# One of sixteen weight-sum units moves from the mixer's last block to its second; the last stores go to two queues by turns

## The chip, the cores and the metric

The kernel runs on one core of one Trainium2 chip. The metric is the device time of one execution in microseconds (us), and for this kernel it is given as the median of three runs. The engines that matter are TensorE (PE in the profile, with its weight loads as PEld), VectorE (DVE), ScalarE (ACT), GpSimd (POOL) and SyncE (SP), which issues nearly all of the kernel's DMA transfers.

## The reference

One layer (DEPTH is 1) of a hybrid encoder runs on 2048 new tokens and 64 tokens of a running stream, in float32, with a model width of 1024:

```python
def hybrid_layer(x, ...):
    h = rmsnorm(x, norm1_w)
    proj = h @ w_in                       # q, k, v, z, a, b and pooling input
    ...                                   # short convolution, SiLU
    o, s_new = gated_delta_chunked(q, k, v, g, beta, s_prev, chunk)
    ...                                   # gated norm of o, multi-scale pooling
    x = x + jnp.concatenate([o_delta, o_pool], axis=-1) @ w_out
    h = rmsnorm(x, norm2_w)
    x = x + (jax.nn.silu(h @ w_gate) * (h @ w_up)) @ w_down
    return x, conv_new, s_new.astype(x.dtype), pool_new
# then y = rmsnorm(x, normf_w)
```

The first half (projection, delta rule, pooling, output projection) is called the mixer here, the second half (gate, up, down) the FFN.

## The kernel before, in words

**Layout.** Everything is held transposed: channels on the 128 partitions, tokens along the free dimension. A dense product is made of three passes: a number is split into a high part (a cast to fp32r on ACT) and a low part (a subtraction on DVE), and high x high, high x low and low x high are summed in PSUM. Each weight tile therefore needs one ACT cast and one DVE subtraction before TensorE can use it. Where a split weight is used again, it is stored in DRAM and loaded back already split.

**The mixer** runs over four blocks of 512 tokens; block 0 also takes the 64 running tokens. In each block the projections of 21 column tiles (`win`) alternate with the delta rule's chains of small products in float16 and float32, one chain per head; the output projection (`wout`) of one block runs inside the next. The output projections of the last two blocks end the mixer.

**The FFN** runs over three blocks of 704 tokens, each as two halves of 352. Gate, up and down use a seven-product scheme of Strassen's kind (buffers `px`, `py`, `pz` for gate and up, `dx`, `dy`, `dz` for down), which needs four sums of quarters of each weight tile: S1, S2, S3 and S4. The 22 hidden tiles are taken in groups of `FGROUPS = (4, 4, 4, 4, 2, 4)`.

**Weight-sum units.** For the down weights `wd` of the four groups named in `PRE[0]` = (1, 2, 3, 5) these sums are made during the mixer by `pre_sums("dn", f, i)`, four units to a group, 16 in all. A unit loads two pieces of `wd` of 128 x 512 (one into the constant tile `poolw`, which the profile calls `consts`, one into a buffer of the `pw` ring, `prdn` in the profile), makes four sums of 128 x 256 on POOL, splits each on ACT and DVE into a spare corner of the block's activation tiles (`h` or `op` in the profile), and stores the four results to `dsd`. The FFN loads them again in `load_down`. The landing place `poolw` exists once, so the next unit's load into it waits for the unit before. All these transfers are issued by SP.

**Where a unit stands.** `plan` is the list of weight tiles in the order in which TensorE uses them, and `with_pres` inserts a unit behind the keys whose places in the block's list are given by `PRE_AT`. `prep()` walks this list a few keys ahead of use (`AHEAD = 3`); a unit is noted at that point but hands no weight over. Blocks 1, 2 and 3 get five, six and five units.

**The order of instructions.** `Machine` records every operation and then issues them by a list schedule with costs of its own: per engine it takes the ready operation with the lowest rank. For TensorE it also holds on to fp32r work before it turns to float16 or float32 products. The order on each engine, and on SP's queue, is fixed in this way before the kernel runs, so that any change to the list of operations can change the order of others.

**The end.** The last FFN block's last down product is done in two halves (`halves`, `ENDS`). `last_norm` follows each: squares on ACT, sums on POOL, a column sum on TensorE, then eight scaled outputs of 128 x 352. In the second half (`i` = 1) six of them are made on DVE and the first two (`SHARE`) on POOL, and each is stored by `nc.sync.dma_start` as soon as it is there.

Of the kernel before, what the change touches and what calls it, by code (L numbers as in the profile page):

```python
# [18 lines left out]
P = 128  # L19
D = 1024  # L20
KT = D // P
# [19 lines left out]
TB2 = NTOK // NB2  # L41
# [10 lines left out]
PRE = (1,2,3,5),(1,2,3,5),(1,2,3)  # L52
# [317 lines left out]
def hybrid_kernel(ctx, tc, a, o):  # L370
    nc = machine = Machine(tc.nc)
# [10 lines left out]
    def mm(out, lhsT, rhs, start, stop, **kw):  # L382
        nc.tensor.matmul(out, lhsT, rhs, start=start, stop=stop, **kw)
        n = 1
        for d in out.shape[1:]:
            n *= d
        cost(n, rhs.dtype)
# [89 lines left out]
    for lo, n in S0:  # L477
        for i in range(2):
            nc.sync.dma_start(out=x0[i][:, :, lo : lo + n],
                              in_=a["xT"][4 * i : 4 * i + 4, :, lo : lo + n].rearrange("k p t -> p k t"))  # L480
# [17 lines left out]
    groups, f0 = [], 0  # L498
# [3 lines left out]
    plan, pres = [], []  # L502
    for gi, (f0, G) in enumerate(groups):
        pres += [("pre", "gu", f, i) for f in range(f0, f0 + G) if f in PRE_GU for i in range(2)]
        pres += [("pre", "dn", f0, m) for m in range(KT // 2) if gi in PRE[0]]

    def with_pres(j, keys):

        out = []
        for i, key in enumerate(keys):  # L510
            out.append(key)
            if i in PRE_AT.get(j, ()) and pres:
                out.append(pres.pop(0))
        return out

    for j in range(NBLK):
        win = [("win", m) for m in range(21)]
        base = len(plan)
        at = 5 + 4 * OUT_AFTER
# [40 lines left out]
    def wtiles(nm, second=False):  # L560

        pool, x = (wq["pool"], "2") if second else (wpool, "")
        at = state["at"]
        return (lambda: pool.tile([P, 512], F32, tag="wraw" + x, name=f"wr{nm}_{at}", bufs=3 if second else 4),
                lambda: pool.tile([P, 2, 512], F32R, tag="wsp" + x, name=f"ws{nm}_{at}", bufs=4))

    def wsplit(t, raw, n=512, eng=None):
        nc.scalar.copy(t[:, 0, :n], raw[:, :n])
        (eng or nc.vector).tensor_tensor(out=t[:, 1, :n], in0=raw[:, :n], in1=t[:, 0, :n].bitcast(F32), op=ALU.subtract)

    def prep():
        key = plan[state["at"]]
        state["at"] += 1
        if key[0] == "pre":
            return pre_sums(*key[1:])
# [83 lines left out]
    def pre_sums(what, f, i):  # L659

        n = 256
        (tl, tr), (ll, lr) = ([t[:, i * n : i * n + n] for i in range(2)] for t in (
            names["poolw"], gp.tile([P, PX], F32, tag="pw", name=f"pr{what}{f}_{i}", bufs=2)[:, :512]))
        if what == "dn":
            for t, m0 in ((tl, i), (ll, i + KT // 2)):
                both = bass.AP(t.tensor, t.offset, [list(t.ap[0]), [1, 2 * n]])
                nc.sync.dma_start(out=both, in_=a["wd"][m0][:, f * P : f * P + 2 * n])
            dst = dsd[f, i]
        else:
            for t, nm, at in ((tl, "wg", 0), (tr, "wg", 512), (ll, "wu", 0), (lr, "wu", 512)):  # L670
                nc.sync.dma_start(out=t, in_=a[nm][f][:, at + i * n : at + i * n + n])
            dst = gpd[f, i]
        gt = nc.gpsimd.tensor_tensor
        spare = B.spare + B.o_spare + (prev.o_spare if prev else [])
        gt(out=lr, in0=lr, in1=ll, op=ALU.add)
        gt(out=ll, in0=tl, in1=ll, op=ALU.subtract)
        gt(out=tl, in0=lr, in1=tl, op=ALU.subtract)
        gt(out=tr, in0=tr, in1=tl, op=ALU.subtract)
        for j, x in enumerate((ll, lr, tl, tr)):
            parts = spare[j % len(spare)]  # L680
            split_w(parts.rearrange("p (q n) -> p q n", q=2), x)
            nc.sync.dma_start(out=dst[j], in_=parts.bitcast(F32))

    def split_w(t, x):

        nc.scalar.copy(t[:, 0], x)
        tt(t[:, 1], x, t[:, 0].bitcast(F32), ALU.subtract)

    def load_down(m, f0, G):

        n, t = G // 2 * P, {}
        for i, nms in enumerate((("11", "12"), ("S3", "S1"), ("S2", "S4"), ("22",))):
            raw, part = wtiles(f"d{nms[0]}", i % 2 == 1)
            part = part()
            if nms[0][0] == "S":
                both = part.rearrange("p q n -> p (q n)").rearrange("p (j q n) -> p j q n", j=2, q=2)
                nc.sync.dma_start(out=both.rearrange("p j q n -> p j (q n)").bitcast(F32),
                                  in_=dsd[f0, m][2 * i - 2 : 2 * i].rearrange("j p n -> p j n"))
                t |= {nm: [both[:, j]] for j, nm in enumerate(nms)}
            else:  # L700
                raw, k = raw(), n * len(nms)
                src = a["wd"][m + (KT // 2 if i else 0)]
                nc.sync.dma_start(out=raw[:, :k], in_=src[:, (f0 + G) * P - k : (f0 + G) * P])
                wsplit(part, raw, k)
                t |= {nm: [part[:, :, j * n : j * n + n]] for j, nm in enumerate(nms)}
        return t

    def prep_down(m, f0, G):
# [214 lines left out]
    at = 0  # L923
# [614 lines left out]
    for k in (4, 5, 6, 7, 0, 1, 2, 3):  # L1538
        t = wpool.tile([P, 512], F32, tag="xc", name=f"od{k}", bufs=XBUFS["xc"])
# [23 lines left out]
    for nm in FH[3:]:  # L1563
        t = f2.tile([P, 4, 2, N2], F32R, tag=f"h{nm}", name=f"hB{nm}")
# [25 lines left out]
    def last_norm(b, ys, i, done):  # L1590

        lo, n = ENDS[i]

        def new(nm):
            return f2.tile([P, 2, N2], F32, tag="hr", name=nm, bufs=3).rearrange("p s n -> p (s n)")[:, :n] if n > N2 else tmp(nm)[:, :n]

        rf = new(f"rf{b}_{i}")
        if i:
            scaled, scales = [], f2.tile([P, 2, N2], F32, tag="hr", name="scales", bufs=3).rearrange("p s n -> p (s n)")
        for k in range(KT):  # L1600
            yield lambda: len(done) > k
            yield 0.8
            sq = rf if k == 0 else new(f"sq{k}nf{b}_{i}")
            act(sq, columns(ys[k], lo, n), AF.Square)
            if i and k < SHARE:
                scaled.append(scales[:, k * n : k * n + n])
                act(scaled[k], columns(ys[k], lo, n), AF.Copy, scale=nfw[:, k : k + 1])
            if 0 < k < KT - 1:
                nc.gpsimd.tensor_tensor(out=rf, in0=rf, in1=sq, op=ALU.add)
        if i == 0:  # L1610
            yield 1.5
        ps = psg(f"rpnf{b}_{i}")[:, :n]
        mm(ps, ones, rf, start=True, stop=False)
        mm(ps, ones, sq, start=False, stop=True)
        act(rf, ps, AF.Ln, bias=epsc, scale=1.0 / D)
        if i:
            act(ps, rf, AF.Exp, scale=-0.5)
        act(rf, rf, AF.Exp, scale=-0.5)
        for k in (*range(SHARE, KT), *range(SHARE)) if i else range(KT):
            y = columns(ys[k], lo, n)  # L1620
            if i and k < SHARE:
                nc.gpsimd.tensor_tensor(out=y, in0=scaled[k], in1=rf, op=ALU.mult)
            else:
                stt(y, y, nfw[:, k : k + 1], ps if i else rf, ALU.mult, ALU.mult)
            nc.sync.dma_start(out=o["yT"][k, :, b * TB2 + lo : b * TB2 + lo + n], in_=y)
            if i == 0:
                yield LAT_STAT

    def columns(y, lo, n):

        return y.rearrange("p s n -> p (s n)")[:, lo : lo + n]

    def tmp(nm):
        return f2.tile([P, N2], F32, tag="t", name=nm, bufs=TB)
# [125 lines left out]
    for op in order:  # L1760
        b = op[1]
        if op[0] == "gu":
            f = op[2]
# [5 lines left out]
            gi = max(g for g, (f0, G) in enumerate(groups) if f0 <= f)  # L1769
# [14 lines left out]
        else:  # L1784
            f0, G = groups[op[2]]
# [5 lines left out]
            for which in halves(b, op[2]) if plain(b, op[2]) else ():  # L1791
                done = []
                if which != (0, 1):
                    Chain(last_norm(b, ys[b], *which, done))
                down(b, op[2], hs, ys[b], which, done)
# [14 lines left out]

MARGIN = {"tensor": 0.25, "vector": 0.1, "scalar": 0.1, "gpsimd": 0.1, "sync": 3.0}
NY, NLEV, NOUT, NX = 3, 3, 5, 3
PRE_AT = {1:(4,8,12,16,20),2:(4,7,10,13,16,19),3:(3,6,9,12,15)}
PRE_GU = ()

XBUFS = {"xs": 4, "xc": 3}
# [138 lines left out]
```

## Time and profile before

| what | value |
|---|---|
| time, median of 3 runs | 2297.03 us (2296.47 to 2297.72) |
| the profiled execution's own time | 2296.7 us |
| its span, first to last instruction | 2294.9 us |
| mean granted TensorE clock | 0.999 |
| PE busy | 2272.2 us (99%), 14518 instructions |
| DVE busy | 1710.1 us (75%) |
| ACT busy | 1342.4 us (58%) |
| POOL busy | 829.9 us (36%) |
| HBM read, written | 403.62 MB, 130.58 MB |
| chain that ended last, share by engine | PE 91%, DVE 4%, DMA 2% |

The span is what the trace covers; the time is 1.8 us longer. In a row of instructions the first figure behind the count is the busy time in us and the second the mean of one in ns; what stands behind the next bar is the idle time of the engine just before these instructions, with what ended it. Almost every instruction is recorded by one helper and so has the line number L285; rows are told apart by their tiles. A row "A <- B" in a view of waits says that A waited for B, with the total in us, the number of times and the longest. Matmuls overlap, so the pitch from one to the next is shorter than the mean duration of one.

Stages on the trace's clock, read from the tiles: block 0 of the mixer 9 to 198 us, block 1 198 to 430, block 2 430 to 650, block 3 650 to about 860, the last output projection to 935, the FFN to 2284, and the last norm and stores to the end.

### The profile page before, as it was taken

How to read it: one execution, taken by the hardware profiler on the slowest of the kernel's cores; microseconds unless marked ns; L12 is line 12 of the kernel's file. 1: busy time of each engine (PE TensorE's matmuls, PEld its weight loads, DVE VectorE, ACT ScalarE, POOL GpSimd, SP SyncE). 2: the span in 40 equal slices, each digit the busy share in tenths (PEclk: the TensorE clock that was granted, in tenths of full speed). 3: DMA queues.
4: the chain of work that ended last, by engine and by line, in shares of the span. 5: the costliest groups of instructions: out<-in, count | busy, mean ns of one | idle time of the engine just before them, and what ended most of it. 6: DMA issues, size and time to landing. Idle time of an engine off the chain costs nothing.

```text
span 2294.9 us, 41549 instructions
## 1 busy us (share of the span) xinstructions
PE 2272.2 (99%) x14518; PEld 2132.5 (93%) x14518; DVE 1710.1 (75%) x3129; ACT 1342.4 (58%) x3039; POOL 829.9 (36%) x893
## 2 busy tenths in 40 slices
PE   8999999999999999999999999999999999999998
PEld 8998898888787888999999999999999999999998
DVE  7989866685678886788888787866667768666576
ACT  6987866684769874565446366554334574353344
POOL 3425342453247450565443245622111453010112
PEclk9999999999999999999999999999999999999999
DMA  8765687578477777877776578789766786667663
GB/s 291 263 185 190 202 293 234 189 236 273 160 243 241 201 213 256 301 257 245 260 265 240 189 253 302 247 261 318 230 199 198 262 272 230 209 216 224 210 194 105
DMA packets 256515, 536.96 MB, mean 234 GB/s; under 512 B 30001, under 2 KB 94001, under 8 KB 256305
## 3 DMA queue, kind: packets, MB, share of 16 engines
q1 hardware_dynamic: 256304, 534.30, 71.0%
q8 instruction: 114, 1.87, 0.3%
q14 instruction: 97, 0.79, 0.1%
HBM read 403.62 MB, written 130.58 MB: 233 GB/s over the span
## 4 chain that ended last, share of the span: by engine, by line
PE 91%; DVE 4%; DMA 2%; issue 1%; ACT 1%; POOL 0%; SPq 0%; DVEq 0%; ACTq 0%; POOLq 0%
PE px L285 22%; PE pp L285 18%; PE pz L285 13%; PE py L285 11%; PE dx L285 9%; PE dy L285 4%; PE d L285 3%; PE dz L285 2%; PE pk_p L285 2%; PE pt_p L285 2%; PE gr_p L285 1%; DVE y L285 1%; PE py_p L285 1%; DMA wnd<-wsp 1%; PE px_p L285 0%
## 5 line engine op out<-in xcount | busy, mean ns | idle before, releaser
L285 PE MATMUL pp<-h,wsp 128*128 128x512 f32 (+1 forms) x2480 | 548.5, 364 | 9.4 <-DVE wsp L285 9.4
L285 PEld LDWEIGHTS pp<-h,wsp 128*128 128x128 f32 x2480 | 401.8, 190 | 58.0 <-ACT wsp L285 9.1
L285 ACT CAST ws<-wr 128x512 fp32r<-128x512 f32 x198 | 122.2, 618 | 168.0 <-PE dx L285 55.4
L285 DVE TENSOR_TENSOR ws<-wr,ws 128x512 fp32r<-128x512 f32 x198 | 172.5, 875 | 31.1 <-ACT ws L285 27.4
L285 POOL TENSOR_TENSOR q<-hr,hr 128x352 f32<-128x352 f32 x52 | 57.9, 1114 | 372.7 <-DVE hr L285 369.9
L285 ACT CAST wsd<-wrd 128x512 fp32r<-128x512 f32 (+1 forms) x120 | 62.7, 526 | 176.7 <-PE dx L285 67.6
L285 DVE TENSOR_TENSOR y<-y,dx 128x352 f32<-128x352 f32 x240 | 121.6, 516 | 58.4 <-PE dx L285 57.6
L285 PE MATMUL pz<-op,wsp 128*128 128x288 f32 (+1 forms) x768 | 163.3, 353 | 0.1
L285 PE MATMUL px<-hA,ws 128*128 128x352 f32 x792 | 145.2, 322 | 0.0
L285 ACT ACTIVATE hr<-g 128x352 f32<-128x352 f32 x132 | 65.6, 497 | 131.2 <-DVE g L285 131.1
L285 PE MATMUL py<-hB,wsS 128*128 128x352 f32 x792 | 141.7, 322 | 0.0
L285 PE MATMUL py<-hA,wsS 128*128 128x352 f32 x792 | 141.3, 322 | 0.0
L285 PE MATMUL pz<-hB,ws 128*128 128x352 f32 x792 | 141.0, 322 | 0.0
L285 ACT CAST TV_p<-pt_p 128x512 f16<-128x512 f32 x192 | 110.2, 588 | 49.0 <-PE pt_p L285 48.6
L285 PE MATMUL px<-hA,wsS 128*128 128x352 f32 x792 | 138.2, 322 | 0.0
L285 PE MATMUL px<-hBT,wsS 128*128 128x352 f32 x792 | 138.0, 322 | 0.2 <-ACT g L285 0.2
L285 PE MATMUL px<-hBT,ws 128*128 128x352 f32 x792 | 137.8, 322 | 0.0
L285 PEld LDWEIGHTS pz<-op,wsp 128*128 128x128 f32 x768 | 120.9, 188 | 12.6 <-DMA wsp<-wod 0.6
L285 PEld LDWEIGHTS px<-hA,ws 128*128 128x128 f32 x792 | 130.0, 188 | 0.1
L285 PE MATMUL dy<-hq,wsdS 128*128 128x352 f32 x672 | 129.7, 322 | 0.3 <-DMA wsdS<-dsd 0.3
L285 PEld LDWEIGHTS py<-hA,wsS 128*128 128x128 f32 x792 | 129.4, 188 | 0.1
L285 PEld LDWEIGHTS px<-hBT,wsS 128*128 128x128 f32 x792 | 128.7, 188 | 0.9 <-ACT g L285 0.9
(697 smaller groups left out, 5771.7 us busy)
## 6 DMA issues: line engine op xcount, KB each, us to landing
wsS<-gS SPq DMA_DIRECT2D x176, 512.0 KB, 4.5
wsp<-wnd SPq DMA_DIRECT2D x126, 512.0 KB, 3.8
gS<-wsS SPq DMA_DIRECT2D x88, 512.0 KB, 5.1
wsdS<-dsd SPq DMA_DIRECT2D x88, 512.0 KB, 4.4
wr<-in_wg_dram SPq DMA_DIRECT2D x132, 256.0 KB, 3.8
wnd<-wsp SPq DMA_DIRECT2D x42, 512.0 KB, 5.5
wrd<-in_wd_dram SPq DMA_DIRECT2D x68, 256.0 KB, 2.8
xd<-x2d SPq DMA_DIRECT2D x96, 176.0 KB, 4.1
```

The lines of the kernel that those rows point to most:

```text
L285: getattr(getattr(self.nc, op.eng), name)(*args, **kw)
```

## The change

Three things change in the code.

1. `PRE_AT`: block 1 gets a sixth unit behind key 22 of its list, and block 3 has four units behind keys 2, 5, 8 and 11 in place of five behind 3, 6, 9, 12 and 15. Block 2 keeps its six places. The units keep their order, so that the first place of block 2 now holds the seventh unit where it held the sixth, and so on. Places count from 0.
2. `pre_sums` and `load_down` are written for groups of two tiles as well as four (`M = 4 // G`). `PRE` is unchanged and names groups of four only, so M is 1 and there are 16 units as before; but a unit now loads its four quarters by four transfers of 128 x 256 instead of two of 128 x 512.
3. In `last_norm`, the second half's stores of odd `k` are issued by ScalarE instead of SyncE.

```diff
-        pres += [("pre", "dn", f0, m) for m in range(KT // 2) if gi in PRE[0]]
+        pres += [("pre", "dn", f0, m) for m in range(KT // 2 * G // 4) if gi in PRE[0]]
...
         if what == "dn":
-            for t, m0 in ((tl, i), (ll, i + KT // 2)):
-                both = bass.AP(t.tensor, t.offset, [list(t.ap[0]), [1, 2 * n]])
-                nc.sync.dma_start(out=both, in_=a["wd"][m0][:, f * P : f * P + 2 * n])
+            G = dict(groups)[f]
+            M, c = 4 // G, G // 2 * P
+            for t, m0, at in ((tl, 0, 0), (tr, 0, c), (ll, KT // 2, 0), (lr, KT // 2, c)):
+                m0, at = m0 + i * M, at + f * P
+                nc.sync.dma_start(out=t.rearrange("p (m c) -> p m c", m=M),
+                                  in_=a["wd"][m0 : m0 + M, :, at : at + c].rearrange("m p c -> p m c"))
             dst = dsd[f, i]
...
     def load_down(m, f0, G):
 
-        n, t = G // 2 * P, {}
+        n, M, t = G // 2 * P, 4 // G, {}
...
-                t |= {nm: [both[:, j]] for j, nm in enumerate(nms)}
+                t |= {nm: [both[:, j, :, e * n : e * n + n] for e in range(M)] for j, nm in enumerate(nms)}
             else:
-                raw, k = raw(), n * len(nms)
-                src = a["wd"][m + (KT // 2 if i else 0)]
-                nc.sync.dma_start(out=raw[:, :k], in_=src[:, (f0 + G) * P - k : (f0 + G) * P])
-                wsplit(part, raw, k)
-                t |= {nm: [part[:, :, j * n : j * n + n]] for j, nm in enumerate(nms)}
+                raw, k, m0 = raw(), n * len(nms), m * M + (KT // 2 if i else 0)
+                src = a["wd"][m0 : m0 + M, :, (f0 + G) * P - k : (f0 + G) * P]
+                nc.sync.dma_start(out=raw[:, : k * M].rearrange("p (m c) -> p m c", m=M), in_=src.rearrange("m p c -> p m c"))
+                wsplit(part, raw, k * M)
+                t |= {nm: [part[:, :, e * k + j * n : e * k + j * n + n] for e in range(M)] for j, nm in enumerate(nms)}
...
-            nc.sync.dma_start(out=o["yT"][k, :, b * TB2 + lo : b * TB2 + lo + n], in_=y)
+            queue = nc.scalar if i and k % 2 else nc.sync
+            queue.dma_start(out=o["yT"][k, :, b * TB2 + lo : b * TB2 + lo + n], in_=y)
...
-PRE_AT = {1:(4,8,12,16,20),2:(4,7,10,13,16,19),3:(3,6,9,12,15)}
+PRE_AT = {1:(4,8,12,16,20,22),2:(4,7,10,13,16,19),3:(2,5,8,11)}
```

## The prediction

> **What bounds the kernel now.** I read the page's totals first, then the table by stage, then what TensorE waits for in the mixer. The totals:
>
> ```profile
> span 2294.9 us, 41549 instructions
> PE 2272.2 (99%) x14518; PEld 2132.5 (93%) x14518; DVE 1710.1 (75%) x3129; ACT 1342.4 (58%) x3039; POOL 829.9 (36%) x893
> ```
>
> TensorE is busy for 2272.2 of 2294.9 us, so all idle time on it comes to 22.7 us. No re-ordering of other engines can win more than that, apart from what re-ordering does to TensorE's own queue. The table by stage says where the 22.7 us lie. The first column is the stretch, then its length, then busy time and instructions of PE, PEld, DVE, ACT and POOL, the granted clock, the DMA engines' busy share and the rate:
>
> ```profile
> core 0: us, PE busy (x) PEld busy (x) DVE busy (x) ACT busy (x) POOL busy (x), PEclk, DMA share, GB/s
> 0.00:9.20 9.20, 0.04 (x1) 0.07 (x1) 3.42 (x11) 5.00 (x11) 2.49 (x9) 1.00 0.81 250
> 198.00:357.00 159.00, 157.97 (x1173) 140.34 (x1172) 123.13 (x265) 112.01 (x287) 64.76 (x82) 1.00 0.73 242
> 357.00:430.00 73.00, 73.00 (x418) 58.25 (x417) 44.34 (x87) 51.70 (x128) 20.84 (x38) 1.00 0.57 188
> 430.00:570.00 140.00, 139.46 (x869) 114.22 (x868) 102.42 (x204) 91.27 (x223) 63.96 (x81) 1.00 0.79 253
> 650.00:773.00 123.00, 123.00 (x776) 99.28 (x774) 106.01 (x204) 101.64 (x259) 75.34 (x98) 1.00 0.75 243
> 773.00:860.00 87.00, 86.45 (x584) 71.01 (x583) 75.44 (x145) 64.04 (x150) 44.79 (x50) 1.00 0.73 204
> 935.00:2284.50 1349.50, 1348.08 (x8394) 1344.78 (x8392) 995.76 (x1683) 680.84 (x1420) 450.16 (x392) 1.00 0.72 237
> 2284.50:2294.90 10.40, 1.57 (x5) 0.59 (x4) 3.56 (x7) 2.01 (x4) 2.48 (x3) 0.82 0.38 139
> ```
>
> The start costs 9.2 us and the end 8.8 (10.40 less 1.57). The whole mixer behind the start loses only a few us: 1.0 in block 1's first part, 0.5 in block 2, nothing at all in 650 to 773, where the five units of the last block run, and 0.55 in the rest of that block. The FFN loses 1.4 us and holds nothing that the change moves. So the stretch that the change relieves has no idle TensorE to give back, and the stretch that receives the unit (357 to 430, behind block 1's fifth unit) has none either. Who ends the mixer's few waits:
>
> ```profile
> PE pk_p L285 <- DVE Sp L285: 0.5, 1, 0.5
> PE pk_p L285 <- ACT vn_p L285: 0.4, 1, 0.4
> PE pt_s L285 <- DVE Yt_s L285: 0.4, 1, 0.4
> PE gb_p L285 <- ACT TV_p L285: 0.2, 1, 0.2
> ```
>
> These are links of the delta rule's chain, each under 0.6 us. The second is the one that a unit caused. The chain of waits shows how:
>
> ```profile
> 533.83 4.58 DMA consts<-in_wd_dram
> 538.47 0.73 POOL prdn L285
> ...
> 542.24 12.16 issue
> ...
> 554.43 0.75 POOL prdn L285
> ...
> 555.21 0.03 ACT h L285
> ...
> 555.52 0.37 ACT vn_p L285
> ...
> 555.93 0.49 PE pk_p L285 x2
> ```
>
> POOL begins a unit's sums late, ACT meets the cast of that sum in its queue and stands before it, and `vn_p`, which TensorE needs, stands behind the cast. This is the one way in which a unit reaches TensorE, and with 16 units it happened once, for 0.4 us.
>
> **The unit that moves.** Its parts have these rows, over the mixer's blocks 1 to 3:
>
> ```profile
> L285 POOL TENSOR_TENSOR prdn<-consts,prdn 128x256 f32<-128x256 f32 x16 | 13.7, 856 | 18.8 <-DMA consts<-in_wd_dram 18.5
> L285 ACT CAST h<-prdn 128x256 fp32r<-128x256 f32 x32 | 12.9, 412 | 6.6 <-POOL prdn L285 2.9 <-PE pp L285 2.3 <-POOL EL_p L285 1.3
> L285 DVE TENSOR_TENSOR h<-prdn,h 128x256 fp32r<-128x256 f32 x32 | 22.6, 707 | 5.4 <-ACT h L285 5.3
> ```
>
> A unit is four sums on POOL (4 x 0.86 = 3.4 us), four casts on ACT (4 x 0.41 = 1.6) and four subtractions on DVE (4 x 0.71 = 2.8), besides its transfers. In the last block (650 to 773) DVE falls from 106.0 to 103.2 of 123 us and ACT from 101.6 to 100.0. In 357 to 430 DVE rises from 44.3 to 47.1 of 73 and ACT from 51.7 to 53.3. Both stay far below the stretch of TensorE work that covers them, so on both sides I cost the move at nothing. If the cover were gone, it would cost at most the 0.4 us of the row above per hit. SP's queue carries the unit's loads and its four stores past the weights' loads of block 1's last keys; those are fetched three keys ahead. In the last block the remaining four stand one to four keys earlier, which puts the first of them ahead of key 3's load; the stretch 650 to 773 starts with `h` just made and shows no idle PE. In block 2 every place stays filled, with another unit of the same size.
>
> **The split loads.** There are 16 units with two more issues each. What one takes on SP, and how long SP stands idle for TensorE in 198 to 860:
>
> ```profile
> L285 SPq DMA_DIRECT2D prdn<-in_wd_dram x16: 328/333/1193, 227.0 to 718.1; - x16
> SPq L285 <- PE pp L285: 233.6, 91, 7.8
> ```
>
> 32 x 0.33 = 10.7 us of a queue that waits 233.6 us for that one cause; the bytes are the same. In a unit the last quarter is issued 2 x 0.33 = 0.7 us later than the second half was. That is 0.7 us more of head-of-line standing on POOL and ACT per unit at worst. It is nothing where the sums wait behind other work, as 15 of 16 did. Bounds: 0 and, if two or three units reach TensorE with all of it, 0.7 x 3 = 2.1 us. I take 0.
>
> **TensorE's own order.** The list schedule is made anew, so the switches between fp32r and the chain's small products may fall differently. Their price:
>
> ```profile
> 807 pieces in order of time: start us, us, what
> 684.27 2.11 PE pp L285 x9
> 883.59 51.00 PE pz L285 x225
> ```
>
> An undisturbed run of 225 goes at 51.00 / 225 = 0.227 us each; a run of nine between small products takes 2.11 us where 9 x 0.227 = 2.04, so a run costs 0.07 us. The first row counts the chain's pieces in 360 to 860; at most half are such runs, 400 x 0.07 = 28 us. Five in a hundred more or fewer are 1.4 us either way. Nothing in the edit favours a sign: I take 0, with 1.4 us either way in the range.
>
> **The last stores.** The end in the timeline, and the same in the table by stage:
>
> ```profile
> 2287.86 3.04 DVE L285 SCALAR_TENSOR_TENSOR y<-y,nw,rpnf 128x352 f32<-128x352 f32 x6 [2.69 <-ACT rpnf L285]
> 2288.43 1.82 POOL L285 TENSOR_TENSOR y<-scales,rf 128x352 f32<-128x352 f32 x2 [3.27 <-ACT rf L285]
> 2288.47 3.82 SPq L285 DMA_DIRECT2D out_yT_dram<-y  x8
> 2289.30:2293.40 4.10, 0.00 (x0) 0.00 (x0) 1.60 (x4) 0.00 (x0) 0.95 (x2) 0.72 0.97 352
> ```
>
> DVE's last product ends at 2287.86 + 3.04 = 2290.90, POOL's at 2290.25. SP issues eight stores in 3.82 us, a pitch of about 0.49, so the last starts at about 2291.88. On two queues the last could start just behind the last product, at 2290.95: 0.93 us earlier. But the DMA engines are 97% busy from 2289.3 to 2293.4 at 352 GB/s; if that is their rate, only 3% of 4.10, 0.12 us, is left. ACT has no work behind its last exponential, so nothing queues behind its stores; an issue by ACT is not in the trace, and I bound it by SP's 0.33 us and, with a store's whole pitch lost, 0.49. That leaves the term between 0.4 us slower (0.49 less 0.12) and 0.93 faster. I take 0.4 faster: packets of eight stores in flight may overlap a little better than a row that is fed one by one, but the 97% row is the nearer.
>
> The Trainium skill, DMA: Bandwidth & Descriptors, section Issuing engines are not separate DMA queues, says that transfers issued by ScalarE, SyncE or GpSimd end on the same 16 DMA engines and interleave, so a second issuer can save issue time alone. By that rule, with the engines as full as the 97% row shows, the term would be 0.1 and the forecast 2296.9; by the issue pitch alone it would be 0.9 and 2296.1. The trace of before, with one issuer only, cannot show which.
>
> **The sum.** Against the profiled execution: 0 for the move, 0 for the loads, 0 for the order, 0.4 off the end: a span of 2294.5 and a time of 2296.3. That execution lies 0.33 us below the median of 2297.03; on the median the forecast is 2296.6 us. 0.2% of this kernel is 4.6 us, about what a measurement of it can tell from no change, so the forecast is within it.
>
> **The rivals.** First, slower: the chain of POOL, ACT and TensorE of 533 to 556 repeats itself. The units of block 2 close up on loads of four issues, one landing place serves all, and POOL has already waited 18.5 us in total for it. If half of the units, eight, hit TensorE with 0.7 us of added loading and the 0.4 of the row above, that is 8 x 1.1 = 8.8 us, and 2305.8. It decides from about four units on (4.6 / 1.1). Against it: one of 16 hit before, and the sixth unit of block 1 goes where TensorE has the least else to wait for. I give it 0.08.
>
> Second, faster: the last block's chains, with DVE and ACT freed, let TensorE run in longer pieces. A sixth of the 28 us of switches is 4.7 us, and with the last stores' 0.4 the time is 2291.9. For it: the last block is the stage with the busiest DVE (86%). Against it: a DVE relief of 2.8 us in 123 is 2%, not a sixth. 0.07.
>
> Third, the change does nothing but re-order: M is 1, there are as many units, and the stores are bound by the engines. Then the end gives the 0.12 us of the 97% row and the time is 2296.9. For it: that row, taken with one issuer. Against it: the pitch of 0.49 us at which SP was the one to wait for. It lies inside the forecast's case and takes 0.35 of its chance. The Trainium skill's rule above would make this the case to expect.
>
> **How the numbers follow.** The forecast's case holds 0.85. Its own range is 2297.03 less 0.9 (end), 1.5 (all four waits of the mixer gone) and 1.4 (switches), so 2293.2; and 2297.03 plus 2.1 (loads), 1.4 and 0.4 less the 1.0 by which all three seldom fall together, so 2299.9. That range leaves out about 2 in 10 with the rivals' 0.15, so it stands as it is. Faster by over 0.2% has 0.07, slower 0.08, within 0.85.
>
> **What would show it.** In the profile after: 24 of the 64 `dsd` stores before block 2, the last one well before 773; `prdn` loaded 32 times where the row above has 16; PE idle under 2 us from 198 to 860; the last store issued near 2291 and the DMA row of the last 4 us still above 0.9. A stall over 1 us on a `pk_p` or `pt_p` behind an ACT cast of a unit would prove the first rival; a `pp` run growing from about 9 to 11 the second. The forecast falls if the median leaves 2292.4 to 2301.6.

## The result, and the profile after

| kernel | median, us | lowest to highest | ratio to before, 95% interval |
|---|---|---|---|
| before, beside the change | 2296.98 | 2295.44 to 2300.24, 21 runs | |
| after | 2300.41 | 2297.42 to 2302.86, 21 runs | 1.0014 [1.0008, 1.0020] |

The change is 3.4 us slower. That is inside the 0.2% called "within" in the prediction, but 0.5 us above its range. The profiled execution after took 2300.38 us, its span 2298.6.

The totals, then the table by stage, with the columns of before (stretch, length, busy time and instructions of PE, PEld, DVE, ACT and POOL, clock, DMA share, GB/s):

```profile
span 2298.6 us, 41639 instructions
PE 2271.4 (99%) x14518; PEld 2130.5 (93%) x14518; DVE 1710.8 (74%) x3129; ACT 1342.8 (58%) x3039; POOL 833.3 (36%) x893
...
198.00:357.00 159.00, 157.54 (x1173) 140.33 (x1172) 125.77 (x267) 113.29 (x289) 66.44 (x83) 1.00 0.71 240
357.00:430.00 73.00, 73.00 (x418) 58.23 (x417) 46.41 (x89) 51.76 (x129) 23.75 (x41) 1.00 0.60 215
430.00:570.00 140.00, 140.00 (x874) 115.35 (x873) 103.56 (x204) 91.88 (x223) 64.46 (x82) 1.00 0.77 258
650.00:773.00 123.00, 122.28 (x753) 97.41 (x752) 100.17 (x195) 99.22 (x252) 72.80 (x95) 1.00 0.73 240
773.00:860.00 87.00, 86.10 (x581) 70.68 (x580) 75.57 (x141) 62.43 (x145) 44.21 (x49) 1.00 0.65 197
935.00:2284.50 1349.50, 1346.29 (x8381) 1342.92 (x8380) 991.32 (x1681) 679.93 (x1418) 449.89 (x390) 1.00 0.71 238
```

The work is the same and TensorE is no busier (2271.4 against 2272.2). Its idle time rose from 22.7 to 27.2 us. The stage that received the unit still has none (73.00 of 73). The stage that gave it away now has 0.72 where it had nothing, 773 to 860 has 0.90 against 0.55, and 935 to 2284.5 has 3.2 against 1.4. Of the rise of 4.5 us, 0.9 lies before 198 us, where TensorE still has the instruction order of before, and 0.7 in the end from 2284.5 on. What TensorE waits for from 198 to 930, and one wait behind it:

```profile
PE ptv_p L285 <- DVE X_p L285: 0.9, 1, 0.9
PE pn_s L285 <- DVE rhs_s L285: 0.5, 1, 0.5
PE px_p L285 <- ACT YtF_p L285: 0.4, 1, 0.4
...
PE px L285 <- ACT g L285: 1.9, 2, 1.5
```

None of these waits for a unit's sum or cast directly. The longest lies at 954.41 us, early in the FFN. The chain of waits of that stretch:

```profile
937.54 7.52 DMA gS<-wsS
...
945.13 0.63 ACT wsS L285
...
952.00 1.50 DVE hr L285
...
954.00 0.36 ACT g L285
...
954.41 1.71 PE px L285 x9
```

A store of 7.52 us holds up a cast, and everything behind it on ACT and DVE comes late. The wait for `YtF_p`, at 697 us, has a unit further back in its chain:

```profile
687.37 1.16 POOL prdn L285
...
692.29 1.10 POOL r L285
...
696.51 0.50 ACT sq5n L285
697.00 0.27 ACT YtF_p L285
```

POOL is busy with a unit's sums, the sums for the norm (`r`) come behind them, ACT's squares wait for those, and `YtF_p` stands behind the squares.

### The profile page after: what moved, and what is told of

It is laid out like the page before. It is cut to its first block, busy times and chain, and to the rows that moved or that the text cites. A ratio compares the mean times of both kernels' runs of the same rounds, so it can differ in the third digit from the quotient of the medians.

```text
span 2298.6 us, 41639 instructions
## 1 busy us (share of the span) xinstructions
PE 2271.4 (99%) x14518; PEld 2130.5 (93%) x14518; DVE 1710.8 (74%) x3129; ACT 1342.8 (58%) x3039; POOL 833.3 (36%) x893
## 4 chain that ended last, share of the span: by engine, by line
PE 87%; DVE 5%; DMA 3%; ACT 2%; issue 1%; POOL 1%; SPq 0%; DVEq 0%; ACTq 0%; POOLq 0%
PE px L285 21%; PE pp L285 16%; PE pz L285 13%; PE py L285 10%; PE dx L285 9%; PE dy L285 4%; PE d L285 3%; PE dz L285 2%; PE pt_p L285 2%; PE pk_p L285 2%; PE gr_p L285 1%; DVE y L285 1%; PE py_p L285 1%; DMA gS<-wsS 0%; ACT E L285 0%
## 5 line engine op out<-in xcount | busy, mean ns | idle before, releaser
L285 PE MATMUL pp<-h,wsp 128*128 128x512 f32 (+1 forms) x2480 | 547.0, 363 | 10.3 <-DVE wsp L285 10.3
L285 PEld LDWEIGHTS pp<-h,wsp 128*128 128x128 f32 x2480 | 401.0, 189 | 58.4 <-ACT wsp L285 9.4
L285 ACT CAST ws<-wr 128x512 fp32r<-128x512 f32 x198 | 122.2, 618 | 170.6 <-PE dx L285 55.0
L285 DVE TENSOR_TENSOR ws<-wr,ws 128x512 fp32r<-128x512 f32 x198 | 172.8, 876 | 34.1 <-ACT ws L285 29.1
L285 POOL TENSOR_TENSOR q<-hr,hr 128x352 f32<-128x352 f32 x52 | 58.2, 1119 | 369.8 <-DVE hr L285 366.9
L285 ACT CAST wsd<-wrd 128x512 fp32r<-128x512 f32 (+1 forms) x120 | 62.5, 526 | 176.3 <-PE dx L285 67.2
L285 DVE TENSOR_TENSOR y<-y,dx 128x352 f32<-128x352 f32 x240 | 121.8, 517 | 57.1 <-PE dx L285 56.0
L285 PE MATMUL pz<-op,wsp 128*128 128x288 f32 (+1 forms) x768 | 162.4, 353 | 0.0
L285 PE MATMUL px<-hA,ws 128*128 128x352 f32 x792 | 145.2, 322 | 0.0
L285 ACT CAST TV_p<-pt_p 128x512 f16<-128x512 f32 x192 | 110.9, 590 | 56.9 <-PE pt_p L285 56.5
L285 ACT ACTIVATE hr<-g 128x352 f32<-128x352 f32 x132 | 65.6, 497 | 131.0 <-DVE g L285 130.7
L285 PE MATMUL py<-hA,wsS 128*128 128x352 f32 x792 | 141.4, 322 | 0.3 <-DVE wsS L285 0.3
L285 PE MATMUL py<-hB,wsS 128*128 128x352 f32 x792 | 141.5, 322 | 0.0
L285 PE MATMUL pz<-hB,ws 128*128 128x352 f32 x792 | 140.8, 322 | 0.0
L285 PE MATMUL px<-hA,wsS 128*128 128x352 f32 x792 | 138.4, 322 | 1.5 <-ACT g L285 1.5
L285 PE MATMUL px<-hBT,wsS 128*128 128x352 f32 x792 | 137.8, 322 | 0.3 <-ACT g L285 0.3
L285 PE MATMUL px<-hBT,ws 128*128 128x352 f32 x792 | 137.7, 322 | 0.0
L285 PEld LDWEIGHTS pz<-op,wsp 128*128 128x128 f32 x768 | 121.0, 188 | 12.1
L285 PEld LDWEIGHTS px<-hA,wsS 128*128 128x128 f32 x792 | 128.9, 188 | 2.0 <-ACT g L285 1.8
L285 PEld LDWEIGHTS px<-hA,ws 128*128 128x128 f32 x792 | 130.0, 188 | 0.1
L285 PEld LDWEIGHTS py<-hA,wsS 128*128 128x128 f32 x792 | 129.4, 188 | 0.6 <-DVE wsS L285 0.6
L285 PE MATMUL dy<-hq,wsdS 128*128 128x352 f32 x672 | 129.6, 322 | 0.1
```

The costliest lines, as they stand in the source:

```text
L285: getattr(getattr(self.nc, op.eng), name)(*args, **kw)
```

## The experiments

Two stretches cover nearly all of TensorE's work, 10 to 960 us (mixer and the FFN's start) and 960 to 2280 (the rest of the FFN). The rows of before and after, with the columns as above:

```profile
10.00:960.00 950.00, 946.68 (x6276) 811.22 (x6276) 726.04 (x1453) 668.94 (x1635) 386.83 (x498) 1.00 0.72 232
960.00:2280.00 1320.00, 1318.58 (x8210) 1315.45 (x8209) 973.20 (x1654) 664.36 (x1387) 435.25 (x381) 1.00 0.71 236
```

```profile
10.00:960.00 950.00, 943.52 (x6261) 806.74 (x6260) 728.04 (x1451) 667.62 (x1631) 388.10 (x498) 1.00 0.69 231
960.00:2280.00 1320.00, 1318.33 (x8209) 1315.32 (x8208) 969.02 (x1652) 665.71 (x1390) 435.98 (x380) 1.00 0.70 236
```

Length less PE busy is the idle time, 3.32 and 1.42 us before, 6.48 and 1.67 after. The table gives the same for each kernel's one profile, and the medians' difference from the runs of before beside it on the same chip. The last column is the order of the FFN's instructions on the four computing engines, compared place by place as the schedule issues them: A is that of before, A' differs from it in 40 places on TensorE, B in 1033, C in 1082, D in 1369, E in 248.

| kernel | median less before's, us | ratio, 95% interval | idle 10 to 960 | idle 960 to 2280 | FFN order |
|---|---|---|---|---|---|
| before | 0 | | 3.32 | 1.42 | A |
| after | +3.4 | 1.0014 [1.0008, 1.0020] | 6.48 | 1.67 | A' |
| e1, stores alone | -0.6 | 0.9998 [0.9989, 1.0007] | 4.07 | 3.22 | A |
| e2, move alone | +5.7 | 1.0025 [1.0016, 1.0035] | 8.92 | 2.39 | B |
| e3, split loads alone | -0.6 | 0.9999 [0.9990, 1.0008] | 4.24 | 1.81 | E |
| e4, change without stores | +3.3 | 1.0015 [1.0006, 1.0024] | 4.63 | 2.35 | A' |
| e5, move, places kept | +4.9 | 1.0022 [1.0013, 1.0030] | 4.98 | 5.03 | C |
| e6, new places alone | 0.0 | 0.9998 [0.9990, 1.0007] | 5.11 | 1.38 | A' |
| e7, schedule made anew | -0.7 | 0.9998 [0.9989, 1.0007] | 4.58 | 1.63 | A |
| e8, e2 and xd late | +2.4 | 1.0012 [1.0003, 1.0020] | 6.63 | 2.42 | D |
| f1, six in block 1 | +2.9 | 1.0012 [1.0003, 1.0020] | 5.80 | 3.04 | B |
| f2, a unit left out | +2.7 | 1.0015 [1.0007, 1.0024] | 5.89 | 6.19 | C |
| f3, six spread | +6.4 | 1.0028 [1.0018, 1.0039] | 9.01 | 3.56 | B |
| f4, move to block 2 | +1.1 | 1.0002 [0.9993, 1.0011] | 3.26 | 3.06 | B |
| g1, after, FFN A | +1.9 | 1.0010 [1.0002, 1.0019] | 5.79 | 1.55 | A |
| g2, before, FFN C | +4.2 | 1.0020 [1.0012, 1.0029] | 3.72 | 5.17 | C |
| g3, e2, FFN A | +3.5 | 1.0015 [1.0007, 1.0024] | 6.89 | 1.68 | A |
| g4, before, xd late, FFN A | -1.5 | 0.9991 [0.9982, 1.0000] | 4.32 | 1.72 | A |
| h1, after, xd late, FFN A | +8.2 | 1.0034 [1.0022, 1.0047] | 10.18 | 1.88 | A |
| h2, g4 and two queues | -2.6 | 0.9989 [0.9980, 0.9998] | 3.51 | 1.46 | A |

One profile carries about 2 us of chance. After and e4 have one order up to the last stores, and their idle times to 960 are 6.5 and 4.6; e4's profile is its fastest run. In the traces every kernel but e7 has the order of before up to 247 us, and yet the idle time from 10 to 198 lies anywhere from 0.7 to 2.1 us. Still, the kernels with 8 us or more of idle time in all are all slower, by 2.4 to 8.2 us.

**The parts by themselves (e1 to e4).**

```diff
 e1, on before
+            queue = nc.scalar if i and k % 2 else nc.sync
 e2, on before
+PRE_AT = {1:(4,8,12,16,20,22),2:(4,7,10,13,16,19),3:(2,5,8,11)}
 e3, on before: the change's pre_sums and load_down
 e4, on after
+            nc.sync.dma_start(out=o["yT"][k, :, b * TB2 + lo : b * TB2 + lo + n], in_=y)
```

Expected of e1: 

> The kernel before with the second half's odd stores on ScalarE's queue and nothing else; all that comes earlier keeps its order. Theory A (two causes: a new order at the seam of mixer and FFN, and a dearer end): about 0.7 us slower, 2297.7, and the stretch from DVE's last product to the end of the span grows from 4.0 to 4.7 us. The prediction's own step: 0.4 us faster. Rival B (the split loads hold up the units): no change. Rival C (all of the 3.4 us comes from the second queue, for instance a longer start or end of the program): 3.4 us slower.

Expected of e2: 

> The kernel before with the new places of the units and nothing else (two loads to a unit, all stores on one queue). Theory A: the move as such costs nothing, and its time is that of whatever order the list schedule makes: 2297 with 1.5 us either way, and no wait over 1 us at the FFN's first gate products, since ScalarE's queue there has the Ln of tile 0 ahead of the four casts, as in the kernel before. Rival B: 2297.0. Rival D (the sixth unit in block 1 is what costs): about 3 us slower, with new PE waits in 357 to 430.

Expected of e3: 

> The kernel before with four loads of 128 x 256 to a unit instead of two of 128 x 512, places and stores as before. Theory A: 2297 with 1.5 us either way. Rival B (the 32 added issues hold up POOL, ACT and then TensorE): 2 to 3 us slower, 2299 to 2300, with more PE waits behind casts of a unit between 198 and 773. Rival D: no change.

Expected of e4: 

> The changed kernel with all last stores on SyncE's queue again; all that comes earlier keeps the changed kernel's order. Theory A: 2.7 us slower than before, 2299.7, with the wait of 1.5 us at the first gate products still there. The prediction's step for the stores would make it 0.4 us slower than the changed kernel, 2300.8. Rival C: as fast as before, 2297.0.

The stores and the split loads are worth nothing that can be measured, and the change without its stores is as slow as with them. The move alone has a higher median than the whole change, with intervals that overlap. So the loss belongs to the move or to what the schedule makes of it. The dearer end of theory A is not seen in e1, whose span ends 4.0 us behind the last product; its 0.7 us lie just inside e1's interval.

**Which part of the move (e5 to e8).** The edits are to `PRE_AT` of before in e5 and e6; in e7 to a latency of the plan; in e8 to e2.

```diff
 e5
+PRE_AT = {1:(4,8,12,16,20,22),2:(4,7,10,13,16,19),3:(3,6,9,12)}
 e6
+PRE_AT = {1:(4,8,12,16,20),2:(4,7,10,13,16,19),3:(2,5,8,11,14)}
 e7
+LAT_G = 4.60
 e8, in Machine.done, with LATE_XD = 4.0
+            + (LATE_XD if p.eng == "sync" and any(nm.startswith("xd") for nm in p.tiles) else 0.0)
```

Expected of e5: 

> The kernel before with a sixth unit in block 1 and the last block's units at 3, 6, 9, 12: the move without the new spacing. What is known so far: the move with the new spacing alone is 5.7 us slower (ratio 1.0025), and TensorE's idle time between 10 and 960 us is 8.9 us there against 3.3 in the kernel before. Theory R (re-plan): a unit's place costs nothing by itself; the list schedule is made anew from block 1 on, and the new order of VectorE, ScalarE and TensorE meets real durations that the plan does not know, so waits appear at other places than the units. By it this kernel is 1 to 6 us slower than before, with TensorE idle for 4.5 to 9 us in 10 to 960, mostly not beside a unit. Rival U (the sixth unit in block 1): 5 to 6 us slower like the full move, with the loss between 357 and 430 us. Rival S (the last block's new places): no difference.

Expected of e6: 

> The kernel before with the last block's five units at 2, 5, 8, 11, 14 in place of 3, 6, 9, 12, 15, and nothing moved between blocks. Orders are the same as before's up to the last block. Theory R: the re-plan reaches only the last block, so only 650 to 960 us can lose; between 0.5 faster and 4 us slower, with new waits of TensorE after 650. Rival U: no difference (ratio 0.9995 to 1.0005). Rival S: 4 to 6 us slower.

Expected of e7: 

> The kernel before with all units and stores where they were, and one latency of the plan changed from 4.53 to 4.60 us, by which the schedule is made anew from block 0 on. No operation is added, removed or moved by hand. Theory R: any new order is likely to be worse than the one before, whose constants fit it: 2 to 7 us slower, TensorE idle for 5 to 10 us in 10 to 960 us. Rivals U and S: no difference beyond 1 us, since no unit has moved; idle 3 to 4 us.

Expected of e8: 

> The move alone (the slowest kernel so far, ratio 1.0025) with one thing more: the plan takes a load of xd as landing 4 us later, so that VectorE's scaling of xd is placed behind later work. In the move alone VectorE stood 3.18 us for an xd that took 9.76 us to land, with X_p behind it, and TensorE waited 2.80 us for X_p at 810 us. Theory H (VectorE's queue stands behind xd's landing): the wait of 2.8 us goes, and the time falls by 2 to 3 us against the move alone, to a ratio of about 1.0013; the idle time of 773 to 860 falls from 2.8 to under 1 us. Theory R without H: the order changes once more and the sum of waits stays at 5 to 9 us, so a ratio of 1.001 to 1.003 with the waits elsewhere.

A schedule made anew costs nothing by itself (e7), nor do new places in the last block (e6). That took down theory R as I had put it, by which any new order loses. The sixth unit of block 1 looked guilty (e5), but not where theory U had it: e5 loses 0.35 us in 357 to 430 and 3.4 us at 1143 to 1170, in the FFN. In e8 the wait for `X_p` is gone (773 to 860 has no idle time, where e2 has 2.8), and the time is about 3 us below e2's, as theory H expected, though the intervals overlap and the FFN's order is another one too; another wait, 2.4 us for `TV_p` at 720, stands in its one profile.

**Giving and receiving apart (f1 to f4).**

```diff
 f1
+PRE_AT = {1:(4,8,12,16,20,22),2:(4,7,10,13,16),3:(3,6,9,12,15)}
 f2, the last unit taken from the list
+    left = pres.pop(0)
+    dsd[left[2:]] = dsd[left[2], left[3] - 1]
+PRE_AT = {1:(4,8,12,16,20),2:(4,7,10,13,16,19),3:(2,5,8,11)}
 f3
+PRE_AT = {1:(4,7,10,13,16,19),2:(4,7,10,13,16,19),3:(2,5,8,11)}
 f4
+PRE_AT = {1:(4,8,12,16,20),2:(4,7,10,13,16,19,22),3:(2,5,8,11)}
```

Expected of f1: 

> Six units in block 1 (a sixth behind key 22), five in block 2 and five in block 3 at before's places: the receiving side without the relief of the last block. So far each kernel with the sixth unit behind key 22 was slower (2.4 to 5.7 us), while new places in the last block alone (ratio 0.9998) and a schedule made anew with no unit moved (0.9998) cost nothing. Theory U (the sixth unit behind key 22 sets it): 3 to 6 us slower, a ratio of 1.0013 to 1.0026. Theory V (four units in the last block set it, with whatever order comes of that): no difference, within 1 us. Theory W (neither: the orders that happen to come out): anything from 1 faster to 6 slower.

Expected of f2: 

> Fifteen units: block 1 and 2 as before, the last block four at 2, 5, 8, 11, and the sixteenth unit left out (its sums aren't computed, the group's third stored unit is read in its place, so part of the down product is another one). The giving side alone, with no unit received anywhere. Theory U: no difference or slightly faster (0 to 1 us: TensorE idles for only 0.6 us in the last block). Theory V: 3 to 6 us slower though work is left out. Theory W: anything from 1 faster to 6 slower.

Expected of f3: 

> The move with block 1's six units at 4, 7, 10, 13, 16, 19, the places of block 2, in place of a sixth behind key 22; the last block as in the change. Theory U in its narrow form (the place behind key 22): no loss, within 1 us. U in its wide form (six units are one too many in block 1): 3 to 6 us slower. Theory V: 3 to 6 us slower. Theory W: anything from 1 faster to 6 slower.

Expected of f4: 

> The move into block 2 in place of block 1: a seventh unit there behind key 22, block 1 with its five, the last block as in the change. Theory U: no loss, within 1 us, since block 1 is as before. Theory V: 3 to 6 us slower. Theory W: anything from 1 faster to 6 slower.

f1 and f3 are slower, as U would have it. But f2, which leaves the last unit's sums out (part of the down product is then another one) and moves nothing into block 1, is slower by about as much as the change. U as recorded doesn't allow that. f4 has the same four units in the last block and shows no loss, which V doesn't allow. That seemed to leave only W, so I compared the orders and found the classes of the table. The waits of TensorE from 1130 to 1180 us sort by them. Each of e2, f1, f3 and f4 (order B) waits 0.8 or 0.9 for `wsS` and 0.3 for `g`; e5 and f2 (order C) share three others; after, e6 and e8 have none there, nor has before. Order C in e5 (f2 has the same three, of 2.0, 1.0 and 0.6 us):

```profile
PE py L285 <- DVE wsS L285: 1.7, 1, 1.7
PE px L285 <- DVE u L285: 1.0, 1, 1.0
PE px L285 <- ACT g L285: 0.7, 1, 0.7
```

The units are long over by then. Their places can act there only through the state from which the list schedule went on. In e5's chain of waits the scaling of an `xd` for the FFN's next block stands on DVE at 1153; that its new place sets these waits is not shown.

**One kernel's FFN order on another's mixer (g1 to g4).** The edit puts the FFN's part of the finished order in the sequence of the kernel named, and leaves the mixer's part where it was. It moves the recording line from L285 to L301.

```diff
+        ffn = [op for op in out if op.order > self.second]
...
+            ffn[place] = named[at]
...
+        out = [next(ffn) if op.order > self.second else op for op in out]
```

Expected of g1: 

> The change with the FFN's instructions in the order of the kernel before (754 places differ, all in the plan's 897 to 1006 us), the mixer in the change's own order. Theory F (the FFN's order carries the loss): the 1.54 us wait at 954 us, ACT's g behind late casts of wsS, goes, and the time falls from a ratio of 1.0014 to 1.0002 to 1.0008. Theory M (the mixer's order carries it): ratio 1.001 to 1.002 as before, TensorE idle for 5 us or more in 10 to 935 us.

Expected of g2: 

> The kernel before, units and mixer in its own order, with the FFN's instructions in the order that e5 and f2 have (up to the plan's 1367 us). Theory F: the waits of 1.0 us at 1143, 0.6 at 1153 and 1.7 to 2.0 at 1169 us appear here too and the kernel is 3 to 4.5 us slower (ratio 1.0013 to 1.002) though no unit moved. Theory M: those waits come from the mixer's lateness and not from the order; less than 1 us.

Expected of g3: 

> The move alone (e2, ratio 1.0025) with the FFN's instructions in the order of the kernel before. Theory F: the waits at 1170 us (0.82 and 0.30) go and the time falls by 1 to 3 us, to a ratio of 1.0012 to 1.002; the rest is the mixer's order (2.8 us behind an xd at 810, 1.9 us in 650 to 773). Theory M: 0.5 us or less, ratio still 1.0023 or more.

Expected of g4: 

> The kernel before, its units where they were, with the plan taking an xd as landing 4 us later (as in e8) and the FFN in the order of the kernel before. Theory H (VectorE's queue standing behind xd's landing costs 0.55 to 1.9 us in each execution of the kernel before): that wait at about 808 us goes and the kernel is 0.5 to 1.5 us faster, ratio 0.9993 to 0.9998, if the mixer's new order brings no wait of its own. If it does, no difference or slower by up to 3 us.

g2 shows the FFN's part. No unit has moved, the mixer is that of before, and TensorE's waits from 1130 to 1180 are e5's to a tenth:

```profile
PE py L301 <- DVE wsS L301: 1.7, 1, 1.7
PE px L301 <- DVE u L301: 1.0, 1, 1.0
PE px L301 <- ACT g L301: 0.7, 1, 0.7
```

Three waits of 3.4 us, and 4.2 us on the median, as theory F expected. By that, order C accounts for f2's loss, and f2 no longer speaks against U. g3 is the same from the other side: without order B the two waits at 1170 go, and e2's 5.7 us become 3.5 (the intervals overlap). g1 stays at 1.0010 and is idle for 5.8 us from 10 to 935, which is theory M's case: the change's own loss is mostly not in its FFN order. What is left in g3 lies in the mixer, and the largest piece of it is one place. VectorE's timeline in e2:

```profile
805.18 0.75 DVE L285 TENSOR_TENSOR Yt_p<-py_p,lmask 128x256 f16<-128x256 f32 x2
809.11 0.59 DVE L285 SCALAR_TENSOR_TENSOR xd<-xd,nw,r 128x352 f32<-128x352 f32 x1 [3.18 <-DMA xd<-x2d]
809.61 0.42 DVE L285 SCALAR_TENSOR_TENSOR X_p<-px_p,TV_p 128x256 f32<-128x256 f32 x1
```

And the chain of waits there:

```profile
799.25 9.76 DMA xd<-x2d
...
810.09 0.44 PE ptv_p L285 x2
```

The queue stands 3.18 us before an `xd` whose load took 9.76 us, and `X_p`, for which TensorE waits 2.8 us at 810, stands behind it. The kernel before has the same spot with another victim:

```profile
806.51 0.58 DVE L285 SCALAR_TENSOR_TENSOR xd<-xd,nw,r 128x352 f32<-128x352 f32 x1 [3.78 <-DMA xd<-x2d]
807.01 0.34 DVE L285 SCALAR_TENSOR_TENSOR Sp<-Sp,EL_p,pk_p 128x128 f32<-128x128 f32 x1
```

There TensorE waits 0.5, 1.9 and 0.7 us (before, e1, g2); in the change's mixer 0.9, 1.0 and 1.9 (after, e4, g1); in the move's 2.8 and 2.1 (e2, g3). Telling the plan that an `xd` lands 4 us later takes the wait away: g4 has none from 795 to 820, and its median is 1.5 us below before's, with an interval that ends at 1.0000.

**The last two.** h1 is after with e8's edit and FFN order A, h2 is g4 with the change's stores.

Expected of h1: 

> The change whole (moved unit, split loads, two queues), with the plan taking an xd as landing 4 us later and the FFN in the order of the kernel before. If the change's loss is the order alone: ratio 0.999 to 1.0005, and no wait of TensorE for X_p at about 802 us. If the move itself costs: 1.001 or more, with waits beside the units.

Expected of h2: 

> g4 (before's places, xd taken as 4 us later, FFN in before's order) with the second half's odd stores on ScalarE. The stores were worth nothing on two queues (0.9998), so the ratio is that of g4, 0.9991, if that gain is real (0.9985 to 0.9997), and 1.0 if it was chance.

h1 (five runs) is outside the first of its expectations. Its time would fit the second, but the waits that its profile shows are not beside the units. From 650 to 860 it is better than after (209.06 of 210 us busy against 208.39), and the wait for `X_p` is 0.2. But between 930 and 960 TensorE waits 6.0 us:

```profile
PE px L301 <- DVE u L301: 1.9, 1, 1.9
PE py L301 <- ACT wsS L301: 1.8, 1, 1.8
PE px L301 <- ACT g L301: 1.6, 2, 0.8
PE py L301 <- DVE wsS L301: 0.7, 1, 0.7
```

Its chain of waits shows SP at the seam of mixer and FFN, held by the mixer's last stores of x2, with the FFN's weights behind them:

```profile
919.49 5.76 DMA x2d<-xc
...
931.65 5.61 DMA x2d<-xc
...
939.15 6.16 DMA wr<-in_wg_dram
...
953.56 4.70 PE px L301 x18
```

So an FFN order that costs nothing behind one mixer goes with waits of 6 us behind another. h1 therefore leaves open whether the move would be free in a good order. h2 gives g4's gain again, in other runs: 2296.09 against 2298.72 us. It is the only kernel whose whole interval lies below 1.

## Why the prediction was right or wrong

**TensorE's own order: the step that failed.** The prediction put 0 there, with 1.4 us either way, and worked the bound out from the price of switches alone, 0.07 us a run. Switches were not it: in the traces the mixer has 408 unbroken runs of `pp` and `pz` products before and 404 after. What a new order changes is what stands ahead of what in ACT's and VectorE's queues, behind a DMA's landing (`xd` at 802) or behind another engine's work (`YtF_p` at 697), and the places seen cost TensorE 0.4 to 2.8 us each. g2, with no unit moved, shows 4.2 us for an order alone, three times the bound of 1.4. The kernels without a sixth unit in block 1 lie between 2.6 us below before and 4.2 above, so a term of 0 should have had bounds of about 4 us on the slow side.

**"The FFN holds nothing that the change moves" was wrong.** The plan goes on from the state in which the mixer leaves it, so the FFN's order changed too: in 40 places of TensorE in the change, 1033 in the move alone. Order C is the dear one; A', the change's own, costs nothing in e6, and g1, which has the change without it, is still 1.9 us slower; so much of the change's loss lies in the mixer.

**The move at nothing: not shown.** All ten kernels with a sixth unit in block 1 are slower than before, with intervals above 1 and by 1.9 to 8.2 us, whatever their FFN order. Of the nine others besides before only the two with order C are. e3 and e7 have new mixer orders from 247 and from 120 us on, without a sixth unit, and lose nothing. f1 and f4 ran beside each other with order B, and f1, which has the sixth unit, has the higher median by 1.8 us. So theory U is a rival that these runs leave standing. Little of the loss lies beside the unit: from 198 to 430 TensorE is idle for 1.3 to 2.6 us in those ten and for 0.9 to 1.4 in the others. Whether the rest is the unit's doing or that of the orders that came with it is open; it would take several mixer orders with six units in block 1 to tell.

**The unit's own work: small, as forecast, but not nothing.** In 357 to 430 TensorE stays fully busy in the profile after. In e2, e5, e8, f1 and g3 it waits there for 0.3 to 0.5 us, for `ktl_p` at about 380, and the chain of waits goes back to the sixth unit's cast on ACT at 366 to 368. As listed, 24 of the 64 `dsd` stores are issued before block 2, the last at 744.1 where it was 772.9, and `prdn` is loaded 32 times. f4 moves a unit into block 2 and shows no difference. The first rival, sums that stand before ACT's queue, came in its mechanism but not in its size: the `vn_p` wait of 0.4 us is gone, and the one for `YtF_p` above, 0.4 us too, has come. PE's idle time from 198 to 860 was to stay under 2 us and is 3.1; it was 2.1 before, so that sign was too narrow as it stood.

**The split loads: right at 0** (e3, 0.9999).

**The last stores: 0.4 faster, measured 0.6 faster by the medians, with an interval from 2.5 faster to 1.6 slower** (e1's ratio on 2298.7), so the forecast's 0.4 and the third rival's 0.12 can't be told apart. The issues did what was forecast:

```profile
2290.83 3.04 DVE L285 SCALAR_TENSOR_TENSOR y<-y,nw,rpnf 128x352 f32<-128x352 f32 x6 [2.69 <-ACT rpnf L285]
...
2291.94 2.36 ACTq L285 DMA_DIRECT2D out_yT_dram<-y  x4
```

ScalarE's last issue ends at 2294.30, next to the last product at 2293.87, yet from the product to the span's end it takes 4.7 us. The five profiles with two issuers have 4.7 (after), 4.5 (g1), 4.1 (h1), 4.0 (e1) and 3.9 (h2) there, the fifteen with one about 4.0. Why two of them are longer is open. The row of the DMA engines says why none is much shorter:

```profile
2292.20:2296.30 4.10, 0.00 (x0) 0.00 (x0) 1.67 (x4) 0.00 (x0) 1.02 (x2) 0.62 0.97 353
```

97% and 353 GB/s, as with one issuer (0.97, 352). The rule of the Trainium skill, DMA: Bandwidth & Descriptors, section Issuing engines are not separate DMA queues, that a second issuer saves issue time alone, agrees with that row.

**The second rival, longer TensorE pieces in the last block,** did not happen in any size: from 650 to 860 there are 599 `pp` and `pz` products in 112 runs before and 601 in 105 after, and the block lost time. (VectorE is not busiest there: it has 87% in block 0, from 9.2 to 198, against 86%.)

**What stays open.** How the change's own 3.4 us divide, and whether the unit or the order causes them. The three profiles of its mixer (after, e4, g1) all have 0.5 us for `rhs_s` at 276, 0.4 for `YtF_p` at 697 and 0.9 to 1.9 for `X_p` at 802, of which before has only the last, as 0.5 to 1.9 for `Sp`. That makes about 1 us more; but e3 has the 0.5 us for `rhs_s` too, and is no slower. The wait of 1.54 at 954 was in after, 0.6 in e6 with the same FFN order, and not in e4. Taking that FFN order away (g1) moves the ratio from 1.0014 to 1.0010, which these intervals don't tell apart. The rest is in executions that no profile caught.

## What to carry to other kernels

Where a list schedule orders a whole program, a change to one operation is a change to all orders behind it, even hundreds of microseconds later; give that its own term, with the spread of a few neutral variants as its bounds. Here an FFN order alone cost 4.2 us. A loss that belongs to the edit must be shown apart from one that belongs to the order: put one kernel's order on the other's work. And look for queue heads that stand before a DMA whose landing the plan has too early: correcting that one estimate gave about 2 us on the kernel before (g4, h2). The correction makes a new order as well, and on the changed kernel it went with a time 8.2 us above before's (h1).

## What the runs showed of the hardware

A load of `xd` of 176 KB lands in 4.1 us at the median of its 96, but took 7.55, 8.69 and 9.76 us at the same spot of the last block in before, after and e2. One kernel's runs spread over 6 us: those of before beside e1 to e4 went from 2294.6 to 2300.85, where its first three lay within 1.3 us. Up to 247 us one and the same order left TensorE idle for 0.7 to 2.1 us from 10 to 198, from execution to execution.
